# Up projections with the tokens stationary: half as many products, and the squared relu transposed on TensorE

## The chip, the core and the metric

The kernel runs on one core of a Trainium2 chip. The metric is the device time of one execution in microseconds (us); lower is better. Of the core's engines the text calls TensorE PE (its weight loads PEld, a row of their own in the profile), VectorE DVE, ScalarE ACT, and SyncE SP, which here issues the weight loads from memory.

## The reference

A decoder trunk of two layers on 256 tokens of 2048 channels, float32. Each layer adds a mixer (layer 0: window attention beside a state space scan; layer 1: dilated attention) and a feed-forward part to the residual. The change touches the feed-forward parts alone:

```python
D_MODEL = 2048
SEQ = 256
D_FF = 4 * D_MODEL

def squared_relu_mlp(h, w_up, w_down):
    u = jnp.einsum('bsd,df->bsf', h, w_up)
    return jnp.einsum('bsf,fd->bsd', jnp.square(jax.nn.relu(u)), w_down)

def reference(...):
    for layer in range(DEPTH):
        h = rms_norm(x, norm_mix[layer])
        ...
        h = rms_norm(x, norm_ffn[layer])
        x = x + squared_relu_mlp(h, w_up[layer], w_down[layer])
    return x
```

## The kernel before

All weights (some 416 MB) stream once through the core. A *unit* is 512 columns of one weight matrix against all 256 tokens; its inner dimension is cut into blocks of 128 rows, the *k-tiles*, and two k-tiles make a *chunk* of 512 KB. Every float32 operand is split into a high and a low part, and a product is the sum of three: high by high, high by low, low by high. For each chunk SP loads `wraw`, ACT copies it to `whi` (`high`), DVE subtracts to get `wlo` (`low`); both run a few chunks ahead (`RAW`, `AHEAD`). The loop in `run` goes through a list of (unit, chunk) in program order, so the order of the products is fixed by the order in which units are made: `up(0)`, `up(1)`, then for each i `up(2i)`, `up(2i+1)`, `down(i-1)`, and the last `down`. Each layer has 16 up units of 16 k-tiles, and 8 down steps of 4 units of 8 k-tiles.

A unit has two forms. In the plain form a block of 128 tokens is stationary and 512 weight columns move: 2 token blocks by 3 products, six products of 512 columns in a k-tile, and the result has the tokens on the partitions. With `flip=True` a block of 128 weight columns is stationary and the 256 tokens move: 4 blocks by 3 products, twelve of 256 columns, and the result has the weight columns on the partitions. In the profile's names the moving operand stands first: `acc<-hThi,whi` is a flipped product, `acc<-whi,hThi` a plain one.

The operand of the tokens is `hThi`/`hTlo` for an up unit (the residual, transposed and times the norm's gain, by `Norm.stripe`) and `uh`/`ul` for a down unit. The norm's factor of each token comes after the product. In a flipped unit the tokens lie along the free axis, so the factor must lie along it too: `Norm` with `rowwise=True` builds `rsb` by a product of a diagonal with ones. In a plain unit the factor is one number per partition (`rs_at`).

Work beside the products (`squared`, `stripe`, attention) is written as generators. `tick` runs before each k-tile and emits their next steps where the charged load allows it; `yield n` asks for a wait of n k-tiles. So a step's place in each engine's queue is set when the program is built. All engines issue in order. PSUM is held by `accs` (two tiles for each unit, two units alive) and `auxs` (four tiles for transposes and small products). Every recorded operation has the line 71, that of the helper which charges the load, so the tiles' names tell the rows apart.

Of the kernel before, what the change touches and what calls it, by code (L numbers as in the profile page):

```python
# [10 lines left out]
AF = mybir.ActivationFunctionType  # L11
# [28 lines left out]
def trunk(ctx: ExitStack, tc: tile.TileContext, x, norm_mix, norm_ffn, w_up, w_down, ab_w_in, ab_q_norm,  # L40
# [14 lines left out]
    spent = {"V": 0.0, "S": 0.0, "PE": 0.0}  # L55

    class Engine:
        """an engine whose instructions are charged roughly, so that work beside the products is spread evenly"""

        def __init__(self, engine, name, fixed, each):  # L60
            self.engine, self.name, self.fixed, self.each = engine, name, fixed, each
# [15 lines left out]
    def slot(name):  # L77
        return slots.tile([128, 4, T], F32R, name=name, tag="slot")
# [7 lines left out]
    def f32(ap):  # L86
        return ap.bitcast(F32)

    # ---------------------------------------------------------------- constants and parameters
    nc.scalar.preload_act_table(AF.Exp)  # L90
    cst = consts.tile([128, C_ALL], F32, name="cst")
    par0 = w4([32, 128], "par0")
# [51 lines left out]
        V.tensor_copy(cwT, p[:, 128:224])  # L144
        yield 4

    # ---------------------------------------------------------------- work beside the weight stream
    tasks = []
    done = set()
    clock = [0]  # L150

    def side(gen, label=None):
        """a step of gen is emitted between products; it yields how many row blocks to wait before the next"""
        tasks.append([clock[0], gen, label])

    def step(forced=False, skip=()):
# [38 lines left out]
    def free(ps):  # L195
        done.add(id(ps))

    # ---------------------------------------------------------------- small arithmetic
    def rsqrt(v, scale, shape, name):
        """1 / sqrt(v * scale + EPS), from a seed by the exponent and three Newton steps"""  # L200
        a = small.tile(shape, F32, name=name + "a", tag="rs_a")
        y = small.tile(shape, F32, name=name + "y", tag="rs_y")
        t = small.tile(shape, F32, name=name + "t", tag="rs_t")
        V.tensor_scalar(a, v, scale, EPS, op0=OP.mult, op1=OP.add)
        V.tensor_scalar(t.bitcast(I32), a.bitcast(I32), 1, None, op0=OP.logical_shift_right)
        V.tensor_scalar(y.bitcast(I32), t.bitcast(I32), -1.0, float(0x5F3759DF), op0=OP.mult, op1=OP.add)
        for _ in range(3):
            V.tensor_tensor(t, y, y, op=OP.mult)
            V.scalar_tensor_tensor(t, t, -0.5, a, op0=OP.mult, op1=OP.mult)
            V.scalar_tensor_tensor(y, t, 1.5, y, op0=OP.add, op1=OP.mult)  # L210
        return y

    def split(hi, lo, src, gain=None):
        """hi + lo = src (* gain), each of float32r's width"""
        if gain is None:
            S.activation(hi, src, AF.Copy)
            V.tensor_tensor(lo, src, f32(hi), op=OP.subtract)
        else:
            S.activation(hi, src, AF.Copy, scale=gain)
            V.scalar_tensor_tensor(lo, src, gain, f32(hi), op0=OP.mult, op1=OP.subtract)  # L220

    # ---------------------------------------------------------------- products with the weights
    units = []

    def unit(segs, ktiles, after, flip=False, needs={}):
        """rows of tokens by weight columns (flip: weight columns by tokens); ktiles: [(row block, operands)]"""
        units.append((segs, ktiles, after, flip, needs))

    def run():
# [90 lines left out]
                pending = after, ps  # L320
        pending[0](pending[1])

    # ---------------------------------------------------------------- the norm of the residual
    class Norm:
        """transposed, gained residual as (hi, lo) blocks; the row factors come after the product"""

        def __init__(self, row, rowwise):
            self.row, self.rowwise = row, rowwise
# [70 lines left out]
        def rsb2(self):  # L399
            return self.rsb[:, None, :].to_broadcast([128, 2, T])  # L400

    # ---------------------------------------------------------------- parts of attention
    def head_norm(nm, ps, n, name):
        """factors of the n heads of 64 columns in ps, the residual's factor included"""
        yield from until(("rs", nm.row))
        sq = w4([128, 2, n * 64], name + "sq")
        for t in range(2):
            S.activation(sq[:, t], ps[t][:, :n * 64], AF.Square, scale=nm.rs_at(t))
        yield 2
        s = small.tile([128, 2, n], F32, name=name + "s", tag="hn_s")  # L410
        V.tensor_reduce(s, sq.rearrange("p t (h e) -> p t h e", e=64), axis=AX.X, op=OP.add)
        y = rsqrt(s, 1.0 / 64, [128, 2, n], name)
        f = small.tile([128, 2, n], F32, name=name + "f", tag="hn_f")
        V.tensor_tensor(f, y, nm.rs[:, :, None].to_broadcast([128, 2, n]), op=OP.mult)
        yield 2
        return f

    def heads_T(nm, ps, gain, name, box):
        """eight heads: norm, then [(two heads, 64), tokens] blocks"""
        f = yield from head_norm(nm, ps, 8, name)  # L420
        qn = w4([128, 2, W], name + "n")
        for t in range(2):
            V.tensor_tensor(qn[:, t].rearrange("p (h e) -> p h e", e=64),
                            ps[t].rearrange("p (h e) -> p h e", e=64),
                            f[:, t, :, None].to_broadcast([128, 8, 64]), op=OP.mult)
        free(ps)
        yield 6
        qT = w4([128, 4, T], name + "T")
        for a in range(2):
            p = aux(name + "p")  # L430
            for b in range(2):
                for t in range(2):
                    PE.transpose(p[:, b * T + t * 128:b * T + (t + 1) * 128],
                                 qn[:, t, (2 * a + b) * 128:(2 * a + b + 1) * 128], ident)
            yield 1
            S.activation(qT[:, 2 * a:2 * a + 2], p.rearrange("p (b t) -> p b t", b=2), AF.Copy,
                         scale=gains[:, gain:gain + 1])
            yield 2
        box.append(qT)
        yield 1  # L440
# [1 line left out]
    BL = ((0, 128), (128, 384))  # L442

    def pair(b, pre, first, qT, kT, vs, hi, lo, mask, mult=None, sink=None, post=None):
        """two heads; blocks (q0,k0) (q1,k0) (q1,k1); kT(b), vs(t, head) pick the keys and values"""
        yield from until(pre)
        if first is not None:
            yield from until(first)
# [63 lines left out]
        split(hi()[:, b], lo()[:, b], o[:, :T])  # L512
        yield 1

    # ---------------------------------------------------------------- the residual's additions
    def add_stripe(ps, j, last=None):
        for t in range(2):
            r = res[:, t, j * W:(j + 1) * W]
# [11 lines left out]

            unit([(w, j * W, W)], ktiles, after, needs=needs if j == 0 else {})

    # ================================================================ layer 0, mixer
    win, wout = ab_w_in[0], ab_w_out[0]
    n0 = Norm(R_MIX, True)
    for j in range(NS):
# [39 lines left out]
        yield 2  # L576

    def steps(ps):
        """dt = softplus(dtx) with log1p(e) = 2 atanh(e / (2 + e)); the decays' prefix sums"""
        st = [128, 2, 32]  # L580
        yield from until(("rs", n0.row))
        V.tensor_scalar(rsh, n0.rs, 0.5, None, op0=OP.mult)
# [79 lines left out]
        unit([(win, AQ + u * W, W)], n0.ktiles(), lambda ps, u=u: swa(u, ps))  # L662

    def conv(ps, ch, y):
        """the causal convolution and 2 * silu of four blocks of channels"""
        pre = w4([128, 4, T], "pre")
        for a in range(2):
            V.tensor_tensor(pre[:, 2 * a:2 * a + 2], ps[a].rearrange("p (b t) -> p b t", b=2), n0.rsb2(), op=OP.mult)
# [40 lines left out]
    dxs, wts = {}, {}  # L709

    def decays(g):
        """(C B^T) * decay of both chunks, for the group's heads, source tokens on the partitions"""
        yield from until("steps")
        wt = []
        for c in range(2):
# [119 lines left out]
        else:  # L835
            unit([(win, AX0 + g * W, W)], n0.ktiles(), lambda ps, g=g: after_x(g, ps), flip=True)

    n1 = Norm(R_FFN, True)
    residual_units(wout, [(i, lambda i=i: (mixh[i // 4], mixl[i // 4], i % 4)) for i in range(24)],
                   {4 * i: ("mix", i) for i in range(6)}, n1)  # L840

    # ================================================================ the feed-forward part
    NB = FF // W

    def mlp(layer, nm, nxt, last=None):
# [2 lines left out]

        def squared(i, ps):
            yield from until(("rs", nm.row))  # L850
            u[i] = slot("uh"), slot("ul")
            ts = []
            for a in range(2):
                t = w4([128, 2, T], "relu")
                V.scalar_tensor_tensor(t, ps[a].rearrange("p (b t) -> p b t", b=2), 0.0, nm.rsb2(),
                                       op0=OP.max, op1=OP.mult)
                ts.append(t)
            free(ps)
            yield 2
            for a in range(2):  # L860
                S.activation(ts[a], ts[a], AF.Square)
                S.activation(u[i][0][:, 2 * a:2 * a + 2], ts[a], AF.Copy)
            yield 2
            for a in range(2):
                V.tensor_tensor(u[i][1][:, 2 * a:2 * a + 2], ts[a], f32(u[i][0][:, 2 * a:2 * a + 2]),
                                op=OP.subtract)
            yield 2

        def after_up(i, ps):
            side(squared(i, ps), ("u", layer, i))  # L870

        def up(i):
            unit([(wu, i * W, W)], nm.ktiles(), lambda ps: after_up(i, ps), flip=True, needs=nm.needs() if i == 0 else {})

        def down(i):
            kts = [(4 * (2 * i + b) + k, (lambda b=b, k=k: u[2 * i + b] + (k,))) for b in range(2) for k in range(4)]
# [12 lines left out]
    n2 = Norm(R_MIX + 16, False)  # L889
    mlp(0, n1, n2)  # L890

    # ================================================================ layer 1, mixer
    wqkv = c_w_qkv[0]
    oh, ol = [None] * 4, [None] * 4

# [43 lines left out]
    for g, i in ((0, 0), (0, 1), (1, 0), (1, 1), (2, 0), (3, 0), (2, 1), (3, 1)):  # L939
        parts[g][i]()  # L940

    n3 = Norm(R_FFN + 16, True)
    residual_units(c_w_o[0], [(i, (lambda i=i: (oh[i // 4], ol[i // 4], i % 4))) for i in range(16)],
                   {4 * g: ("o", g) for g in range(4)}, n3)

# [14 lines left out]


def _shapes():
    """arrays that follow from the shapes: identity, prefix triangle, masks, branch counts"""
    import numpy as np
    c = np.zeros((128, C_ALL), np.float32)
    i = np.arange(128)
# [35 lines left out]
```

## Time and profile before

| | |
|---|---|
| time, median of 3 executions | 2336.72 us (2336.21 to 2336.78) |
| profiled execution, first to last instruction (span) | 2334.6 us |
| PE busy | 2322.0 us, 99%, 14137 products |
| PEld busy | 2064.2 us, 88% |
| DVE busy | 1430.6 us, 61% |
| ACT busy | 1094.5 us, 47% |
| read from memory | 420.64 MB, 181 GB/s over the span |

The times are those of whole executions; the profiled one is given by its span, which leaves out what lies before the first and after the last instruction. A busy share is a mean over the whole span. Products on PE are pipelined, so the duration of one row overlaps the next: the rate is read from the starts.

### The profile page before, as it was taken

How to read it: one execution, taken by the hardware profiler on the slowest of the kernel's cores; microseconds unless marked ns; L12 is line 12 of the kernel's file. 1: busy time of each engine (PE TensorE's matmuls, PEld its weight loads, DVE VectorE, ACT ScalarE, POOL GpSimd, SP SyncE). 2: the span in 40 equal slices, each digit the busy share in tenths (PEclk: the TensorE clock that was granted, in tenths of full speed). 3: DMA queues.
4: the chain of work that ended last, by engine and by line, in shares of the span. 5: the costliest groups of instructions: out<-in, count | busy, mean ns of one | idle time of the engine just before them, and what ended most of it. 6: DMA issues, size and time to landing. Idle time of an engine off the chain costs nothing.

```text
span 2334.6 us, 35702 instructions
## 1 busy us (share of the span) xinstructions
PE 2322.0 (99%) x14137; PEld 2064.2 (88%) x14137; DVE 1430.6 (61%) x2188; ACT 1094.5 (47%) x1411; POOL 8.4 (0%) x20
## 2 busy tenths in 40 slices
PE   8999999999999999999999999999999999999999
PEld 7999988899899899899888778778989989989897
DVE  6779986555555555555566776755555555555554
ACT  5565545444344444444454555554444444344342
POOL 1000000000000000000000000000000000000000
PEclk9999999999999999999999999999999999999999
DMA  7546655565666656656555545456665665656654
GB/s 232 161 144 190 188 164 189 188 183 181 191 189 188 191 184 188 192 187 189 189 180 182 157 152 176 155 165 183 184 191 181 190 191 186 191 185 186 191 188 161
DMA packets 229223, 425.09 MB, mean 182 GB/s; under 512 B 15620, under 2 KB 26160, under 8 KB 229056
## 3 DMA queue, kind: packets, MB, share of 16 engines
q1 hardware_dynamic: 218976, 416.34, 57.7%
q10 hardware_dynamic: 9568, 6.34, 0.9%
q8 instruction: 110, 1.80, 0.3%
q14 instruction: 57, 0.47, 0.1%
q0 software_dynamic: 512, 0.15, 0.0%
HBM read 420.64 MB, written 2.13 MB: 181 GB/s over the span
## 4 chain that ended last, share of the span: by engine, by line
PE 99%; DMA 0%; DVE 0%; ACT 0%; SPq 0%; issue 0%; ACTq 0%
PE acc L71 94%; PE sc L71 1%; PE o L71 1%; PE pT L71 1%; PE yp L71 1%; PE xT L71 1%; DMA wraw<-in_ab_w_in_dram 0%; PE qp L71 0%; PE yo L71 0%; PE kp L71 0%; PE yT L71 0%; PE xtok L71 0%; PE hst L71 0%; DVE wlo L71 0%; ACT whi L71 0%; PE cbp L71 0%
## 5 line engine op out<-in xcount | busy, mean ns | idle before, releaser
L71 DVE TENSOR_TENSOR wlo<-wraw,whi 128x1024 fp32r<-128x1024 f32 (+1 forms) x792 | 962.5, 1218 | 685.1 <-PE acc L71 557.7
L71 ACT ACTIVATE whi<-wraw 128x1024 fp32r<-128x1024 f32 (+1 forms) x792 | 835.8, 1056 | 1085.4 <-PE acc L71 981.9
L71 PE MATMUL acc<-hThi,whi 128*128 128x256 f32 x2432 | 692.5, 285 | 0.0
L71 PE MATMUL acc<-hThi,wlo 128*128 128x256 f32 x2432 | 688.1, 283 | 0.0
L71 PE MATMUL acc<-hTlo,whi 128*128 128x256 f32 x2432 | 688.1, 283 | 0.0
L71 PEld LDWEIGHTS acc<-hThi,whi 128*128 128x128 f32 x2432 | 466.6, 192 | 4.0 <-issue 3.3
L71 PEld LDWEIGHTS acc<-hTlo,whi 128*128 128x128 f32 x2432 | 466.7, 192 | 1.6 <-issue 1.0
L71 PEld LDWEIGHTS acc<-hThi,wlo 128*128 128x128 f32 x2432 | 466.6, 192 | 0.0
L71 PE MATMUL acc<-whi,uh 128*128 128x512 f32 x1024 | 399.1, 390 | 0.0
L71 PE MATMUL acc<-wlo,uh 128*128 128x512 f32 x1024 | 398.5, 389 | 0.0
L71 PE MATMUL acc<-whi,ul 128*128 128x512 f32 x1024 | 398.4, 389 | 0.0
L71 PE MATMUL acc<-whi,hThi 128*128 128x512 f32 (+1 forms) x608 | 243.8, 401 | 2.8 <-ACT hThi L71 2.8
L71 PE MATMUL acc<-whi,hTlo 128*128 128x512 f32 (+1 forms) x608 | 235.9, 388 | 0.3 <-DVE hTlo L71 0.3
L71 PE MATMUL acc<-wlo,hThi 128*128 128x512 f32 (+1 forms) x608 | 235.3, 387 | 0.0
L71 PEld LDWEIGHTS acc<-whi,ul 128*128 128x128 f32 x1024 | 192.2, 188 | 40.1
L71 PEld LDWEIGHTS acc<-whi,uh 128*128 128x128 f32 x1024 | 192.3, 188 | 39.3
L71 PEld LDWEIGHTS acc<-wlo,uh 128*128 128x128 f32 x1024 | 192.3, 188 | 39.2
L71 DVE TENSOR_TENSOR res<-acc,res 128x512 f32<-128x512 f32 x144 | 98.8, 692 | 78.1 <-PE acc L71 78.1
L71 PEld LDWEIGHTS acc<-whi,hThi 128*128 128x128 f32 x608 | 115.4, 190 | 29.5 <-issue 5.9
L71 PEld LDWEIGHTS acc<-whi,hTlo 128*128 128x128 f32 x608 | 115.1, 189 | 24.4 <-DVE hTlo L71 0.9
L71 PEld LDWEIGHTS acc<-wlo,hThi 128*128 128x128 f32 x608 | 115.4, 190 | 21.5 <-issue 1.0
L71 PE MATMUL acc<-whi,mixh 128*128 128x512 f32 x192 | 75.6, 394 | 0.0
(198 smaller groups left out, 1444.5 us busy)
## 6 DMA issues: line engine op xcount, KB each, us to landing
wraw<-in_w_up_dram SPq DMA_DIRECT2D x256, 512.0 KB, 3.7
wraw<-in_w_down_dram SPq DMA_DIRECT2D x256, 512.0 KB, 4.4
wraw<-in_ab_w_in_dram SPq DMA_DIRECT2D x96, 512.0 KB, 3.7
wraw<-in_c_w_qkv_dram SPq DMA_DIRECT2D x96, 512.0 KB, 3.8
wraw<-in_ab_w_out_dram SPq DMA_DIRECT2D x48, 512.0 KB, 3.9
wraw<-in_c_w_o_dram SPq DMA_DIRECT2D x32, 512.0 KB, 3.9
wt<-cumd ACTq DMA_DIRECT2D x8, 512.0 KB, 6.9
res<-in_x_dram SPq DMA_DIRECT2D x4, 512.0 KB, 5.0
```

Source lines behind the costliest of these rows:

```text
L71: return f(out, *a, **k)
```

## The change

Up units lose `flip=True`. The squared relu is then formed with the tokens on the partitions: ACT applies relu and the token's factor to both PSUM tiles, DVE squares, PE transposes the result in two groups of four 128x128 blocks into `uT`, and ACT and DVE split that into `uh` and `ul`. The norms ahead of the feed-forward parts no longer build `rsb`.

```diff
-    n1 = Norm(R_FFN, True)
+    n1 = Norm(R_FFN, False)
...
         def squared(i, ps):
             yield from until(("rs", nm.row))
-            u[i] = slot("uh"), slot("ul")
-            ts = []
-            for a in range(2):
-                t = w4([128, 2, T], "relu")
-                V.scalar_tensor_tensor(t, ps[a].rearrange("p (b t) -> p b t", b=2), 0.0, nm.rsb2(),
-                                       op0=OP.max, op1=OP.mult)
-                ts.append(t)
+            r = w4([128, 2, W], "relu")
+            for t in range(2):
+                S.activation(r[:, t], ps[t], AF.Relu, scale=nm.rs_at(t))
             free(ps)
             yield 2
+            V.tensor_tensor(r, r, r, op=OP.mult)
+            yield 3
+            u[i] = slot("uh"), slot("ul")
             for a in range(2):
-                S.activation(ts[a], ts[a], AF.Square)
-                S.activation(u[i][0][:, 2 * a:2 * a + 2], ts[a], AF.Copy)
-            yield 2
-            for a in range(2):
-                V.tensor_tensor(u[i][1][:, 2 * a:2 * a + 2], ts[a], f32(u[i][0][:, 2 * a:2 * a + 2]),
-                                op=OP.subtract)
-            yield 2
+                p = aux("uT")
+                for b in range(2):
+                    for t in range(2):
+                        PE.transpose(p[:, b * T + t * 128:b * T + (t + 1) * 128],
+                                     r[:, t, (2 * a + b) * 128:(2 * a + b + 1) * 128], ident)
+                yield 1
+                p = p.rearrange("p (b t) -> p b t", b=2)
+                split(u[i][0][:, 2 * a:2 * a + 2], u[i][1][:, 2 * a:2 * a + 2], p)
+                yield 2
...
-            unit([(wu, i * W, W)], nm.ktiles(), lambda ps: after_up(i, ps), flip=True, needs=nm.needs() if i == 0 else {})
+            unit([(wu, i * W, W)], nm.ktiles(), lambda ps: after_up(i, ps), needs=nm.needs() if i == 0 else {})
...
-    n3 = Norm(R_FFN + 16, True)
+    n3 = Norm(R_FFN + 16, False)
```

On PE, in the up unit that follows the fifth one of layer 0 (`up(5)`), the products of one k-tile stood like this before; one token operand moves against blocks of `whi` and `wlo`:

```order
L71 MATMUL acc_6502<-hThi_4184,whi_6410 128x256
L71 MATMUL acc_6502<-hTlo_4185,whi_6410 128x256
L71 MATMUL acc_6502<-hThi_4184,wlo_6436 128x256
L71 MATMUL acc_6503<-hThi_4184,whi_6410 128x256
L71 MATMUL acc_6503<-hTlo_4185,whi_6410 128x256
L71 MATMUL acc_6503<-hThi_4184,wlo_6436 128x256
```

In the changed kernel the same unit, around the end of its sixth k-tile, reads (`relu` is the squared relu of the fifth unit, `cst` the identity):

```order
L71 MATMUL acc_6048<-whi_6027,hThi_4428 128x512
L71 MATMUL acc_6048<-wlo_6041,hThi_4428 128x512
L71 MATMUL acc_6048<-whi_6027,hTlo_4429 128x512
L71 MATMUL uT_6097<-cst_81,relu_6049 128x128 x4
L71 MATMUL acc_6047<-whi_6027,hThi_4428 128x512
L71 MATMUL acc_6047<-wlo_6041,hThi_4428 128x512
L71 MATMUL acc_6047<-whi_6027,hTlo_4429 128x512
```

A k-tile's twelve products have become six, and the first four transposes stand behind 36 products of the unit that follows; the second four stand 18 products later, and so it is after all 32 up units. All other instructions of PE keep their place between the products, but for the two `rsb` pairs that go.

On ACT, around the same unit's end, before (a `relu` row here squares what DVE made):

```order
L71 ACTIVATE whi_6538<-wraw_6438 128x1024
L71 ACTIVATE relu_6506<-relu_6506 128x512
L71 ACTIVATE uh_6504<-relu_6506 128x512
L71 ACTIVATE relu_6508<-relu_6508 128x512
L71 ACTIVATE uh_6504<-relu_6508 128x512
L71 ACTIVATE whi_6572<-wraw_6468 128x1024
```

and in the changed kernel:

```order
L71 ACTIVATE whi_6045<-wraw_5989 128x1024
L71 ACTIVATE relu_6049<-acc_5901,rs32_4979 128x512
L71 ACTIVATE relu_6049<-acc_5902,rs32_4979 128x512
L71 ACTIVATE whi_6068<-wraw_6007 128x1024
L71 ACTIVATE whi_6087<-wraw_6025 128x1024
L71 ACTIVATE whi_6112<-wraw_6043 128x1024
L71 ACTIVATE uh_6095<-uT_6097 128x512
L71 ACTIVATE whi_6132<-wraw_6066 128x1024
L71 ACTIVATE uh_6095<-uT_6134 128x512
L71 ACTIVATE whi_6157<-wraw_6085 128x1024
```

ACT still has four instructions for the unit, but two of them now wait for PE's transposes, each with a `whi` queued behind it.

On DVE, before (the first two rows read the unit's PSUM tiles):

```order
L71 SCALAR_TENSOR_TENSOR relu_6506<-acc_6260,rsb_5194 128x512
L71 SCALAR_TENSOR_TENSOR relu_6508<-acc_6261,rsb_5194 128x512
L71 TENSOR_TENSOR wlo_6534<-wraw_6408,whi_6500 128x1024
L71 TENSOR_TENSOR wlo_6568<-wraw_6438,whi_6538 128x1024
L71 TENSOR_TENSOR ul_6505<-relu_6506,uh_6504 128x512
L71 TENSOR_TENSOR ul_6505<-relu_6508,uh_6504 128x512
```

and in the changed kernel:

```order
L71 TENSOR_TENSOR wlo_6064<-wraw_5989,whi_6045 128x1024
L71 TENSOR_TENSOR relu_6049<-relu_6049 128x1024
L71 TENSOR_TENSOR wlo_6083<-wraw_6007,whi_6068 128x1024
L71 TENSOR_TENSOR wlo_6108<-wraw_6025,whi_6087 128x1024
L71 TENSOR_TENSOR ul_6096<-uT_6097,uh_6095 128x512
L71 TENSOR_TENSOR wlo_6128<-wraw_6043,whi_6112 128x1024
L71 TENSOR_TENSOR ul_6096<-uT_6134,uh_6095 128x512
```

The reading of PSUM moved to ACT, one square of 1024 columns came in, and the two subtractions moved behind the transposes, with one `wlo` between them.

## Rows read from the trace of the kernel before

**Rows 1.** The page: span, PE and PEld (busy, share, count), PE and its granted clock over 40 slices (tenths), the bytes from memory and their rate, and the shares of the chain of work that ended last.

```profile
span 2334.6 us, 35702 instructions
PE 2322.0 (99%) x14137; PEld 2064.2 (88%) x14137; DVE 1430.6 (61%) x2188; ACT 1094.5 (47%) x1411; POOL 8.4 (0%) x20
PE   8999999999999999999999999999999999999999
PEclk9999999999999999999999999999999999999999
HBM read 420.64 MB, written 2.13 MB: 181 GB/s over the span
PE 99%; DMA 0%; DVE 0%; ACT 0%; SPq 0%; issue 0%; ACTq 0%
```

**Rows 2.** The chain of work that ended last, its last piece: start, length, what, count.

```profile
1636.76 693.90 PE acc L71 x4416
```

**Rows 3.** The page's costliest groups: count, busy us and mean ns of one, idle time before them and its main releaser.

```profile
L71 DVE TENSOR_TENSOR wlo<-wraw,whi 128x1024 fp32r<-128x1024 f32 (+1 forms) x792 | 962.5, 1218 | 685.1 <-PE acc L71 557.7
L71 ACT ACTIVATE whi<-wraw 128x1024 fp32r<-128x1024 f32 (+1 forms) x792 | 835.8, 1056 | 1085.4 <-PE acc L71 981.9
```

**Rows 4.** PE in order of time (start us, duration us): the borders of a block of two up units (714.08 to 760.15) and of the down step behind it (760.15 to 803.70), layer 0.

```profile
713.85 0.39 PE L71 MATMUL acc<-whi,ul 128*128 128x512 f32 x1
714.08 0.28 PE L71 MATMUL acc<-hThi,whi 128*128 128x256 f32 x1
...
760.03 0.28 PE L71 MATMUL acc<-hThi,wlo 128*128 128x256 f32 x1
760.15 0.40 PE L71 MATMUL acc<-whi,uh 128*128 128x512 f32 x1
...
803.47 0.39 PE L71 MATMUL acc<-whi,ul 128*128 128x512 f32 x1
803.70 0.28 PE L71 MATMUL acc<-hThi,whi 128*128 128x256 f32 x1
```

**Rows 5.** Groups of instructions by form within 714.0 to 760.1, then within 760.12 to 803.6: count, busy us and mean ns of one. One of three products is shown of each; the other two have the same counts and means.

```profile
L71 PE MATMUL acc<-hThi,wlo 128*128 128x256 f32 x128 | 36.2, 283 | 0.0
...
L71 PE MATMUL acc<-whi,uh 128*128 128x512 f32 x64 | 24.9, 389 | 0.0
```

**Rows 6.** Busy time of the engines in stretches (PE, PEld, DVE, ACT, POOL, each with a count; granted clock, DMA share, GB/s): the same up block, the same down step, the projections of layer 1's attention.

```profile
714.00:760.10 46.10, 46.10 (x386) 46.06 (x385) 23.45 (x23) 19.14 (x20) 0.00 (x0) 1.00 0.60 183
760.10:803.60 43.50, 43.50 (x194) 36.03 (x194) 25.86 (x27) 19.21 (x20) 0.00 (x0) 1.00 0.62 194
1208.40:1512.00 303.60, 303.60 (x1498) 243.38 (x1497) 208.76 (x554) 160.56 (x232) 0.00 (x0) 1.00 0.53 167
```

**Rows 7.** PE in order of time in layer 1's attention, where plain units with `hThi` run and two groups of four transposes (`qp`) stand between their products.

```profile
1458.93 0.39 PE L71 MATMUL acc<-whi,hTlo 128*128 128x512 f32 x1
1459.16 0.60 PE L71 MATMUL qp<-cst,qn 128*128 128x128 f32 x4
1459.52 0.48 PE L71 MATMUL acc<-whi,hThi 128*128 128x512 f32 x1
...
1463.51 0.39 PE L71 MATMUL acc<-whi,hTlo 128*128 128x512 f32 x1
1463.73 0.60 PE L71 MATMUL qp<-cst,qn 128*128 128x128 f32 x4
1464.09 0.47 PE L71 MATMUL acc<-whi,hThi 128*128 128x512 f32 x1
...
1472.13 0.39 PE L71 MATMUL acc<-whi,hTlo 128*128 128x512 f32 x1
```

**Rows 8.** Stretches between those groups, of instructions on `acc` alone (PE, PEld, DVE, ACT with counts; clock, DMA share, GB/s); the count of PEld is that of the products between.

```profile
1459.40:1463.70 4.30, 4.18 (x18) 3.30 (x18) 0.00 (x0) 0.00 (x0) 1.00 0.69 248
1463.70:1472.30 8.60, 8.41 (x37) 6.68 (x36) 1.28 (x2) 0.00 (x0) 1.00 0.63 186
```

**Rows 9.** The group of those transposes by form, mean ns of one.

```profile
L71 PE MATMUL qp<-cst,qn 128*128 128x128 f32 x48 | 7.2, 272 | 0.0
```

**Rows 10.** PE in order of time around the product that builds `rsb` in layer 0's feed-forward part.

```profile
511.26 0.28 PE L71 MATMUL acc<-hThi,wlo 128*128 128x256 f32 x1
511.38 0.59 PE L71 MATMUL rsb<-diag,ones 128*128 128x256 f32 x2
511.62 0.47 PE L71 MATMUL acc<-hThi,whi 128*128 128x256 f32 x1
511.93 0.28 PE L71 MATMUL acc<-hTlo,whi 128*128 128x256 f32 x1
512.04 0.28 PE L71 MATMUL acc<-hThi,wlo 128*128 128x256 f32 x1
```

**Rows 11.** Tiles' instructions (count, duration ns min/median/max): DVE reading PSUM and ACT in the old squared relu, DVE on 1024 columns in SBUF, ACT with a token's factor from PSUM, DVE's subtraction.

```profile
L71 DVE SCALAR_TENSOR_TENSOR relu<-acc,rsb x64: 681/692/693, 513.5 to 2243.6; 128x512 f32<-128x512 f32 x64
L71 ACT ACTIVATE relu<-relu x64: 611/614/616, 515.7 to 2245.6; 128x512 f32<-128x512 f32 x64
L71 ACT ACTIVATE uh<-relu x64: 632/632/633, 516.4 to 2246.3; 128x512 fp32r<-128x512 f32 x64
L71 DVE TENSOR_TENSOR ul<-relu,uh x64: 681/685/690, 519.3 to 2247.9; 128x512 fp32r<-128x512 f32 x64
L71 DVE TENSOR_TENSOR z<-z,dx x4: 1218/1218/1225, 232.9 to 360.4; 128x1024 f32<-128x1024 f32 x4
L71 ACT ACTIVATE v<-acc,rs x10: 348/690/690, 42.7 to 1515.3; 128x512 f32<-128x512 f32 x8, 128x128 f32<-128x128 f32 x2
```

**Rows 12.** DVE in order of time at the end of an up unit (its products end at the middle of the block of Rows 4, 737.11): start, duration, idle before and its releaser.

```profile
736.59 1.41 DVE L71 SCALAR_TENSOR_TENSOR relu<-acc,rsb 128x512 f32<-128x512 f32 x2 [0.88 <-PE acc L71]
```

**Rows 13.** Loads from memory: count, KB each, median us from issue to landing.

```profile
wraw<-in_w_up_dram SPq DMA_DIRECT2D x256, 512.0 KB, 3.7
wraw<-in_w_down_dram SPq DMA_DIRECT2D x256, 512.0 KB, 4.4
```

**Rows 14.** The start of layer 1's feed-forward part: its first products on PE, then DVE's last piece of the norm's last stripe, which the thirteenth k-tile reads.

```profile
1612.26 0.28 PE L71 MATMUL acc<-hThi,whi 128*128 128x256 f32 x1
...
1624.80 0.87 DVE L71 SCALAR_TENSOR_TENSOR hTlo<-xT,gains,hThi 128x256 fp32r<-128x256 f32 x2
```

## The prediction

> **What bounds the kernel now.** I read the page first: engines, slices, chain. PE is busy 99% of the span in nearly every slice, its granted clock stands at the upper of its two levels, 2.4 GHz, throughout, and the chain that ended last is PE for 99% [rows 1]. "Busy" alone would not tell whether PE waits, since durations overlap, so I looked at the pieces of the chain: from 1636.76 to the end 4416 products follow one another for 693.90 us with nothing else in between [rows 2]. The other engines wait for PE: ACT's `whi` 981.9 us, DVE's `wlo` 557.7 us [rows 3]. So in the feed-forward parts the time is the number of PE instructions times the distance between their starts, and the change is to be priced in that coin.
>
> That distance is read from the borders of blocks. Two up units, 384 flipped products of 256 columns (three groups of 128), take 714.08 to 760.15, 46.07 us: 0.1200 us each. The down step behind them, 192 products of 512 columns (three groups of 64), takes 43.55 us: 0.2268 us each [rows 4, 5]. The mean durations (283 and 389 ns) are no rates: they overlap. A product of twice the columns costs 0.2268 where two cost 0.2400, so each product carries some 0.013 us that doesn't depend on its columns. Put another way: 256 more columns cost 0.1068 us, which is 256 columns at 2.4 GHz, and 0.0132 us of each start is left over.
>
> **The change, part by part.**
>
> *The products.* There are 2 x 16 up units of 16 k-tiles. Flipped they are 12 products per k-tile, 6144 in all: 6144 x 0.1200 = 737.1 us. Plain they are 3072: 3072 x 0.2268 = 696.8 us. Gain 40.3 us. The columns that pass through PE are the same in both; the gain is all in the 3072 starts that go. That the plain form with `hThi` stationary runs at the same distance as the down step is seen in layer 1's attention: between two groups of transposes 18 and 36 products (the counts of PEld in [rows 8]) lie within 4.58 and 8.62 us [rows 7], which leaves no room for a slower one.
>
> The Trainium skill speaks against this term: its page "TensorE: Matmul & The Clock Gate", section "Back-to-back issue gap", gives an isolated distance of N/2.4 + 2.5 ns. By it two products of 256 cost 218.3 ns and one of 512 costs 215.8, so the gain would be an estimated 7.7 us and, with the other terms below, the kernel some 22 us slower. The trace doesn't agree: its fixed part is 13 ns, not 2.5, on both widths [rows 4].
>
> *The transposes.* Each unit now has two groups of four, 64 groups. The nearest rows could hardly be nearer: `qp`, four transposes of 128x128 float32 between plain products of the same form [rows 7]. One is shown with a mean of 272 ns [rows 9], yet four are through in 0.36 us, from 1459.16 to the next product at 1459.52. The price is what the group adds to the stream, including the first products behind it, whose distance is longer (1463.73, 1464.09). From 1458.93 to 1463.51 there are 18 products and one group: 4.58 - 18 x 0.2268 = 0.50 us. From 1463.51 to 1472.13 there are 36 and one: 8.62 - 8.16 = 0.46 us. A unit will have just such a pair, 0.96 us; 32 of them cost 30.5 us. Bounds: all as the cheaper, 29.1; all as the dearer, 31.9 us; further out, 0.60 us for each, the busy time in the group's own row [rows 7], 38.4 us.
>
> *The row factor.* Two `rsb` pairs go. Around one, three products take 0.78 us (511.26 to 512.04) where they take 0.36, so a pair costs 0.42 us [rows 10]; 0.8 us for both layers. That relu no longer waits for `rsb` shortens no chain, since PE waited for neither.
>
> *ACT and DVE.* ACT per unit: before 2 x 614 + 2 x 632 = 2.5 us; after, four of 512 columns from PSUM, the nearest row 690 ns (`v`), 2.8 us. DVE per unit: before 2 x 692 + 2 x 685 = 2.75 us; after, a square at 1.22 us and two subtractions at 0.69: 2.6 us [rows 11]. Both are priced at nothing: in an up block DVE has 23.45 of 46.10 us and ACT 19.14 [rows 6], and in the attention stage PE stays full with DVE at 209 of 304 us.
>
> *The new wait.* PE now waits for the squared relu before each first group; behind that wait stand all its products. When is the square ready? DVE's `relu` began at 736.59, before its unit's end at 737.11 [rows 12], because it needs only the half that is done first, some 0.2 us after that half. In the plain form the first token block is done three products earlier than the second, so ACT's two instructions end about 0.2 + 0.69 = 0.9 us after the unit. DVE has one `wlo` (1.22 us, [rows 3]) ahead of the square; if that starts at the unit's end the square is done about 2.5 us after it. The first transposes stand 36 products later, 8.2 us. Margin 5.7 us. Behind the first `uh`, which waits for the transposes (to about 8.8 us), stands a `whi` for the eighth chunk of this unit, needed after 7 x 2.72 = 19.0 us; with 0.69 us for `uh` and 1.06 of its own [rows 3, 11] it is done at 10.6. Behind `ul` stands a `wlo` for the seventh chunk, needed at 16.3 us and done by about 11.4. So I take zero, and keep a late square as a rival.
>
> *Next in line.* If PE speeds up, does the weight stream follow? A unit of 4.19 MB will take 96 x 0.2268 + 0.96 = 22.7 us, 185 GB/s, between the 183 of an up block and the 194 that the down step had with PE full [rows 6]; in one short stretch it reached 248 [rows 8]. Loads land after 3.7 to 4.4 us [rows 13], less than two chunks. At a layer's start, the norm's last stripe is done at 1624.80 + 0.87 = 1625.67, and its first reader will come 12 x 6 x 0.2268 = 16.3 us after 1612.26, at 1628.6 [rows 14]: 2.9 us are left, and the stripe's steps are placed by k-tiles and move forward with them.
>
> **The sum.** -40.3 - 0.8 + 30.5 = -10.6 us against the span of 2334.6: 2324.0 us. The median lies 2.1 us above the span, so I predict 2326.1 us, 0.45% less. With the bounds of the transposes, 29.1 to 31.9, it is 2324.7 to 2327.5; the borders are read to 0.01 us, so each distance is uncertain by some 0.1 us in 384 products, which over the 16 blocks is 1 to 2 us more on either side.
>
> **The rivals.** 0.2% of the time, 4.7 us, is about what a measurement of this kernel can tell from no change.
>
> 1. *The columns are the price* (slower). If the time went by columns streamed and not by starts, the products would gain nothing and the groups would be added: 2336.7 - 0.8 + 30.5 = 2366 us. The mechanism decides from a fixed part below (30.5 - 0.8) / 3072 = 9.7 ns per product; the rows give 13 [rows 4], and the two widths run under the same clock. A fixed part of a fifth of the measured one would end here too; 2%. (The Trainium skill's rule from "TensorE: Matmul & The Clock Gate" is a case of it; with its 7.7 us of gain the time would be an estimated 2358.7.)
>
> 2. *PE waits at the first group* (slower). The place is `uT`, on the square of `relu`; it decides from 10.6 / 32 = 0.33 us of wait per unit, which needs the square 6.0 us later than I worked out. A square that slips by three chunks of 2.72 us, as when DVE's queue is held by a `wlo` whose `wraw` is late, gives 2.5 us in each unit: 2326 + 80 = 2406 us. Against it: DVE itself waited 557.7 us for PE [rows 3]. 4%.
>
> 3. *The weights don't follow* (no change). If up units could not run faster than the 183 GB/s they ran at, the transposes would fill PE's waits and the blocks would keep their 46.07 us: 2335.9 us. For it: the mean of 181 is near [rows 1]. Against it: 194 with PE full in the next block [rows 6]. 4%.
>
> 4. *Dear groups* (no change). At 0.60 us each: 2326.1 + 7.9 = 2334.0 us. For it: the first group behind a wait from another engine is the dearer of the two in rows 7. Against it: both `qp` groups have such a wait behind them and are counted in full. 5%.
>
> **How the numbers follow.** My forecast has 85%. Rivals 3 and 4 end within 0.2% (2332.0 to 2341.4) and 1 and 2 above it. So faster 0.85, the same 0.09, slower 0.06. The range is that of the forecast, with the uncertainty of the distances and a part of the way to the dear groups: 2322.5 to 2330.
>
> **What the trace will show.** Right: up products `acc<-whi,hThi` 0.227 us apart; a block of two up units from its first product to the down step's first in about 45.5 us instead of 46.07; two `uT` rows of four per unit, each adding 0.46 to 0.50 us; no idle time of PE put down to DVE `relu`; granted clock at the top level; the chain of PE still without a piece of another engine in the feed-forward parts. Wrong: idle time before `uT`, products further apart than 0.227 us in up units, ACT's `whi` waiting for DMA instead of PE, or groups near 0.6 us.

## The result and the profile after

The changed kernel takes 2324.63 us (median of 5, 2324.33 to 2325.13), the kernel before, run beside it, 2336.21 (2336.09 to 2336.78). The ratio is 0.9950 with a 95% interval of 0.9937 to 0.9962; 11.6 us less. 2326.1 was forecast, with a range of 2322.5 to 2330. In a later set of runs it took 2324.81 us beside 2336.28.

The page of the changed kernel, the lines that answer to [rows 1] and [rows 3]:

```profile
span 2322.7 us, 30056 instructions
PE 2310.5 (99%) x11317; PEld 1928.3 (83%) x11317; DVE 1425.4 (61%) x2150; ACT 1100.2 (47%) x1411; POOL 8.4 (0%) x20
PEclk9999999999999999999999999999999999999999
PE acc L71 93%; PE uT L71 1%; PE sc L71 1%; PE o L71 1%; PE pT L71 1%; PE yp L71 1%; PE xT L71 1%; DMA wraw<-in_ab_w_in_dram 0%; PE qp L71 0%; PE yo L71 0%; PE kp L71 0%; PE xtok L71 0%; PE yT L71 0%; PE hst L71 0%; DVE wlo L71 0%; ACT whi L71 0%
...
L71 DVE TENSOR_TENSOR wlo<-wraw,whi 128x1024 fp32r<-128x1024 f32 (+1 forms) x792 | 962.3, 1218 | 611.3 <-PE acc L71 524.1
L71 ACT ACTIVATE whi<-wraw 128x1024 fp32r<-128x1024 f32 (+1 forms) x792 | 836.7, 1058 | 950.6 <-PE acc L71 831.9
```

PE has 2820 instructions fewer, which is -3072 products, -4 for `rsb` and +256 transposes. It is as full as before, at the same granted clock, and `wlo` and `whi` still wait for PE (524.1 and 831.9 us, [rows 3]: 557.7 and 981.9). So the bound has not moved; its work has become shorter. Each product has a load of its own (x11317 in both rows), and PEld fell from 88% to 83% with them.

PE in order of time: the borders of a block of two up units (from 711.61) and of the down step behind it (756.08 to 800.54), where [rows 4] has 46.07 and 43.55 us, and in between two groups of transposes:

```profile
711.61 0.39 PE L71 MATMUL acc<-whi,hThi 128*128 128x512 f32 x1
...
739.94 0.39 PE L71 MATMUL acc<-whi,hTlo 128*128 128x512 f32 x1
740.17 0.60 PE L71 MATMUL uT<-cst,relu 128*128 128x128 f32 x4
740.52 0.48 PE L71 MATMUL acc<-whi,hThi 128*128 128x512 f32 x1
...
744.50 0.39 PE L71 MATMUL acc<-whi,hTlo 128*128 128x512 f32 x1
744.73 0.60 PE L71 MATMUL uT<-cst,relu 128*128 128x128 f32 x4
745.08 0.48 PE L71 MATMUL acc<-whi,hThi 128*128 128x512 f32 x1
...
755.85 0.39 PE L71 MATMUL acc<-whi,hTlo 128*128 128x512 f32 x1
756.08 0.39 PE L71 MATMUL acc<-whi,uh 128*128 128x512 f32 x1
...
800.54 0.39 PE L71 MATMUL acc<-whi,hThi 128*128 128x512 f32 x1
```

The blocks now take 44.47 and 44.46 us, 192 products and two groups each: up and down cost PE the same. The two groups of the block's second unit stand in the down step. From 739.94 to 744.50 there are 18 products and one group: 4.56 - 18 x 0.2267 = 0.48 us, as at `qp` in [rows 7].

What the new wait has to spare is seen on ACT and DVE around the end of the first of those units, 711.61 + 96 x 0.2267 = 733.37 (start, duration, in brackets the idle time before and its releaser):

```profile
732.89 1.37 ACT L71 ACTIVATE relu<-acc,rs 128x512 f32<-128x512 f32 x2 [0.98 <-PE acc L71]
...
733.40 1.22 DVE L71 TENSOR_TENSOR wlo<-wraw,whi 128x1024 fp32r<-128x1024 f32 x1 [1.50 <-PE acc L71]
734.54 1.22 DVE L71 TENSOR_TENSOR relu<-relu 128x1024 f32<-128x1024 f32 x1
```

ACT's relu ends 0.9 us and the square 2.4 us after the unit. The transposes follow at 740.17, 6.8 us after it and not 8.2: here the text ahead of the result was wrong, on which more below.

### The profile page after: what moved, and what is told of

Read it like the earlier page. It is cut to its first block, busy times and chain, and to the rows that moved or that the text cites. A ratio compares the mean times of both kernels' runs of the same rounds, so it can differ in the third digit from the quotient of the medians.

```text
span 2322.7 us, 30056 instructions
## 1 busy us (share of the span) xinstructions
PE 2310.5 (99%) x11317; PEld 1928.3 (83%) x11317; DVE 1425.4 (61%) x2150; ACT 1100.2 (47%) x1411; POOL 8.4 (0%) x20
## 4 chain that ended last, share of the span: by engine, by line
PE 99%; DMA 0%; DVE 0%; ACT 0%; SPq 0%; issue 0%; ACTq 0%
PE acc L71 93%; PE uT L71 1%; PE sc L71 1%; PE o L71 1%; PE pT L71 1%; PE yp L71 1%; PE xT L71 1%; DMA wraw<-in_ab_w_in_dram 0%; PE qp L71 0%; PE yo L71 0%; PE kp L71 0%; PE xtok L71 0%; PE yT L71 0%; PE hst L71 0%; DVE wlo L71 0%; ACT whi L71 0%
## 5 line engine op out<-in xcount | busy, mean ns | idle before, releaser
L71 DVE TENSOR_TENSOR wlo<-wraw,whi 128x1024 fp32r<-128x1024 f32 (+1 forms) x792 | 962.3, 1218 | 611.3 <-PE acc L71 524.1
L71 ACT ACTIVATE whi<-wraw 128x1024 fp32r<-128x1024 f32 (+1 forms) x792 | 836.7, 1058 | 950.6 <-PE acc L71 831.9
L71 PE MATMUL acc<-whi,hThi 128*128 128x512 f32 (+1 forms) x1632 | 645.9, 396 | 2.6 <-ACT hThi L71 2.6
L71 PE MATMUL acc<-whi,hTlo 128*128 128x512 f32 (+1 forms) x1632 | 634.7, 389 | 0.3 <-DVE hTlo L71 0.3
L71 PE MATMUL acc<-wlo,hThi 128*128 128x512 f32 (+1 forms) x1632 | 634.0, 388 | 0.0
L71 PEld LDWEIGHTS acc<-whi,hThi 128*128 128x128 f32 x1632 | 307.6, 188 | 68.0 <-issue 5.8
L71 PEld LDWEIGHTS acc<-whi,hTlo 128*128 128x128 f32 x1632 | 307.4, 188 | 64.8 <-DVE hTlo L71 0.9
L71 PEld LDWEIGHTS acc<-wlo,hThi 128*128 128x128 f32 x1632 | 307.9, 189 | 60.2 <-issue 1.0
L71 PE MATMUL acc<-hThi,whi 128*128 128x256 f32 x384 | 112.3, 293 | 0.0
L71 PE MATMUL acc<-hThi,wlo 128*128 128x256 f32 x384 | 108.5, 283 | 0.0
L71 PE MATMUL acc<-hTlo,whi 128*128 128x256 f32 x384 | 108.5, 283 | 0.0
L71 PEld LDWEIGHTS acc<-hThi,whi 128*128 128x128 f32 x384 | 73.5, 191 | 3.4 <-issue 3.3
```

The source lines that it names most:

```text
L71: return f(out, *a, **k)
```

## The experiments

Ten are variants of the changed kernel, and one is the changed kernel once more. The first four price its terms.

**The count of starts: `e1_halves`.** Each plain up product is cut in two. Up units get this branch, the others keep theirs:

```diff
+                if flip == "cut":
+                    for t in range(2):
+                        h, l = xh[:, t * 128:(t + 1) * 128], xl[:, t * 128:(t + 1) * 128]
+                        for c0, c1 in ((0, 256), (256, W)):
+                            o, wh, wl = ps[t][:, c0:c1], hi[:, k, c0:c1], lo[:, k, c0:c1]
+                            PE.matmul(o, h, wh, start=first and c0 == 0, stop=False, skip_group_check=True)
+                            PE.matmul(o, h, wl, start=False, stop=False, skip_group_check=True)
+                            PE.matmul(o, l, wh, start=False, stop=last, skip_group_check=True)
```

> The changed kernel, but each up product of 512 weight columns is cut into two of 256: the tokens stay stationary, the stationary block is loaded anew for each half, and the count of starts is the old one (12 per k-tile). My theory (a start costs 13 ns beside its columns, whichever operand is stationary): 0.120 us from start to start, 3072 starts more at 13.3 ns, 40.9 us more than the changed kernel's 2324.6: 2365.5 us. Rival (the gain comes from which operand is stationary, tokens instead of weight columns, not from the count): no change, 2324.6 us.

Measured: 2364.57 us (2364.03 to 2364.66), 39.9 us above the changed kernel. The distance is that of the old flipped products:

```profile
719.95 0.28 PE L71 MATMUL acc<-whi,hThi 128*128 128x256 f32 x1
720.07 0.28 PE L71 MATMUL acc<-wlo,hThi 128*128 128x256 f32 x1
720.19 0.28 PE L71 MATMUL acc<-whi,hTlo 128*128 128x256 f32 x1
```

So which operand stands still plays no part; the count of starts does. (Each start here has a weight load of its own, so the 13 ns are those of a start with its load.) That the products' term is some 40 us, and why, is shown for these widths.

The groups of transposes are a little cheaper among these halves. Two products ahead of a group, with the groups:

```profile
748.63 0.28 PE L71 MATMUL acc<-whi,hTlo 128*128 128x256 f32 x1
748.75 0.60 PE L71 MATMUL uT<-cst,relu 128*128 128x128 f32 x4
...
753.37 0.28 PE L71 MATMUL acc<-whi,hTlo 128*128 128x256 f32 x1
753.50 0.60 PE L71 MATMUL uT<-cst,relu 128*128 128x128 f32 x4
```

Between the two products lie 36 starts and one group: 4.74 - 36 x 0.120 = 0.42 us, 0.05 less than among products of 512. 36 of the 64 groups stand in up units (the others in down steps), so the 39.9 us hold a saving of some 1.8 us, and the starts alone cost an estimated 41.7 us.

**How far the rule reaches: `e2_uneven`.** The same with `((0, 384), (384, W))`.

> As the run with two halves, but cut into 384 and 128 columns: the same count of starts, the same columns. My theory (fixed part plus 0.4167 ns per column): 173.3 + 66.7 = 240.0 ns per pair, as with the halves, 2365.5 us. Rival (a start can't follow the one before it faster than a weight load allows; the transposes' starts, 0.109 us apart with 128 columns each, are that floor): 173.3 + 109 = 282 ns per pair against 226.7, 3072 x 56 ns = 171 us more than the changed kernel: 2496 us.

Measured: 2510.36 us (2510.11 to 2510.91). My theory fell, by 145 us, and the rival came within 14. PE in order of time (start, duration):

```profile
559.69 0.39 PE L71 MATMUL acc<-whi,hThi 128*128 128x384 f32 x1
559.91 0.34 PE L71 MATMUL acc<-wlo,hThi 128*128 128x384 f32 x1
560.09 0.34 PE L71 MATMUL acc<-whi,hTlo 128*128 128x384 f32 x1
560.27 0.23 PE L71 MATMUL acc<-whi,hThi 128*128 128x128 f32 x1
560.33 0.28 PE L71 MATMUL acc<-wlo,hThi 128*128 128x128 f32 x1
560.44 0.27 PE L71 MATMUL acc<-whi,hTlo 128*128 128x128 f32 x1
560.55 0.40 PE L71 MATMUL acc<-whi,hThi 128*128 128x384 f32 x1
560.78 0.34 PE L71 MATMUL acc<-wlo,hThi 128*128 128x384 f32 x1
```

Busy times in a stretch of it (PE, PEld, DVE, ACT, POOL, then granted clock, DMA share, GB/s):

```profile
560.00:572.00 12.00, 12.00 (x85) 12.00 (x84) 5.21 (x5) 3.84 (x5) 0.00 (x0) 1.00 0.47 135
```

The products of 384 columns stand 0.175 us apart, as the fixed part and the columns say (160 + 13 ns). For those of 128 the rule gives 0.067 us: the first is followed after 0.06, the other two only after 0.11, and the product of 384 after them needs 0.23 before the next may start. The six take 0.86 us where three of 512 take 0.68; 1024 x 0.183 = 187 us, the measured rise. PEld is busy for all of the 12 us. That alone doesn't tell that the loads set the pace, since it was as busy in the old up block at 0.120 us (46.06 of 46.10 us [rows 6]). What speaks for it is that the distance no longer goes with the moving columns. In layer 0's mixer, products of 64 columns (`yp`) run one behind the other, each with a load of a full 128x128 block, here in the changed kernel's trace:

```profile
214.79 1.89 PE L71 MATMUL yp<-xdt,wt 128*128 128x64 f32 x16
216.49 0.37 PE L71 MATMUL acc<-hThi,whi 128*128 128x256 f32 x1
```

16 starts take 1.70 us, 0.106 each, where 13 ns and the columns would give 0.04. Nor is a start as such held to 0.11, since one followed after 0.06. The loads are the reading that fits both; no run changed the loads alone, so it is argued and not shown. The Trainium skill, page "TensorE: Matmul & The Clock Gate", section "LDWEIGHTS (loading the stationary operand)", gives P / 1.2 ns for P columns, an estimated 107 ns for 128; the 0.11 us here agree. So the "13 ns beside the columns" of the prediction holds from 256 to 512 columns and may not be carried below: with a load for each product, 256 columns at 0.120 us stand just above that floor.

**The groups: `e3_no_transposes` and `e4_twice`.**

```diff
-                p = aux("uT")
-                for b in range(2):
-                    for t in range(2):
-                        PE.transpose(...)
                 yield 1
-                p = p.rearrange("p (b t) -> p b t", b=2)
+                p = r[:, a].rearrange("p (b t) -> p b t", b=2)
```

> The changed kernel without its 256 transposes: the split reads the squared relu as it lies (this leaves the transposition out of the computation). My theory: the 64 groups cost 0.472 us each in PE's stream, 30.2 us, so 2294.4 us. Rival (the transposes partly fill time in which PE would wait for ACT or DVE): a smaller fall, above 2300 us, with idle time of PE or longer distances between products in the trace.

Measured: 2293.91 us (2293.66 to 2294.45), 30.7 us less than the changed kernel. The last piece of the chain of work is unbroken again, as in [rows 2]:

```profile
1598.55 689.56 PE acc L71 x3042
```

So the transposes fill no idle time; all of their price is on the path.

```diff
-                for b in range(2):
+                for b in (0, 1, 0, 1):
                     for t in range(2):
                         PE.transpose(...)
```

> The changed kernel with every group of four transposes made twice in a row (eight to a group, the second four overwrite the first with the same). My theory: a transpose costs its distance of 0.109 us and a group some 0.036 us beside that, so 256 more cost 27.9 us: 2352.5 us. Rival (the price is one per group, for leaving and entering the stream of products, as the longer distances behind a group suggest): clearly less, near the changed kernel's 2324.6 us. Rival (a transpose costs its duration, 272 ns): 69.6 us more, 2394 us.

Measured: 2352.10 us (2351.73 to 2352.88), 27.5 us above the changed kernel, 0.107 us for each of 256 more transposes. A group of eight in its place:

```profile
751.14 0.40 PE L71 MATMUL acc<-whi,hTlo 128*128 128x512 f32 x1
751.38 1.03 PE L71 MATMUL uT<-cst,relu 128*128 128x128 f32 x8
752.17 0.47 PE L71 MATMUL acc<-whi,hThi 128*128 128x512 f32 x1
```

From the group's start to the next product 0.79 us, against 0.35 for four: the price goes by transposes, at 0.11 us each. Neither the duration (272 ns, [rows 9]) nor a price per group alone is what is paid.

**Place: `e5_at_12`, `e6_at_6`, `e9_at_12_true`.** These move the first transposes nearer to the unit's end. The names of the first two are wrong, since I had counted a unit of 288 columns as a full one: they stand at 6 and at 0 products, the third at 12. The edit of `e5_at_12` is shown; `e6_at_6` has no `yield` in either place, `e9_at_12_true` has `yield 1` in both.

```diff
             free(ps)
-            yield 2
             V.tensor_tensor(r, r, r, op=OP.mult)
-            yield 3
+            yield 1
```

> The changed kernel with its first transposes 12 products behind the unit's end instead of 36 (relu and square are emitted in one step, the transposes one k-tile later). The squared relu is done 2.2 to 2.4 us after the unit's end, and 12 products take 2.72 us. My theory (a group costs its 0.472 us wherever it stands, as long as its operand is ready): 2324.6 us, no idle time of PE. Rival (PE pays something for a wait that is met only just): up to 0.5 us per unit, 16 us, 2341 us.

Measured: 2353.78 us (2353.08 to 2354.28), against both expectations, because of the miscount. At 6 products the transposes are reached 1.36 us after the unit's end (at 831.65, so the unit ended at 830.29), and the square is done at 832.45, 2.2 us after it. DVE's square and PE in order of time, with the idle time before and its releaser:

```profile
831.22 1.23 DVE L71 TENSOR_TENSOR relu<-relu 128x1024 f32<-128x1024 f32 x1 [2.39 <-ACT relu L71]
831.42 0.39 PE L71 MATMUL acc<-whi,hTlo 128*128 128x512 f32 x1
832.50 0.66 PE L71 MATMUL uT<-cst,relu 128*128 128x128 f32 x4 [0.68 <-DVE relu L71]
832.91 0.47 PE L71 MATMUL acc<-whi,hThi 128*128 128x512 f32 x1
```

1.08 us lie between the starts instead of 0.23. With the transposes a little further apart that is 0.9 us in each of 32 units, 29 us: the measured rise, and what was worked out for 6 products in the next run's expectation.

> The changed kernel with its first transposes 6 products (1.36 us) behind the unit's end, before the squared relu is done (2.2 to 2.4 us). My theory: PE stands for the difference, about 0.95 us, in each of 32 units, and nothing else fills it, 30 us more: 2355 us, with idle time before uT put down to DVE's relu. Rival (the products behind the transposes are pulled ahead, or ACT and DVE, which run ahead, make it up): 2324.6 us.

Measured: 2418.89 us (2417.71 to 2419.72), 94 us above the changed kernel; at 0 products, so the number in the text was for another place. The wait itself is 2.43 - 0.23 = 2.20 us; with 0.06 us for transposes that stand a little further apart behind it, as in `e5_at_12`, it comes to some 72 us in 32 units. The other 22 us come from the clock. Three stretches around one of these waits, busy times of the engines with the granted clock third from the end:

```profile
557.00:562.20 5.20, 3.16 (x16) 2.35 (x15) 2.38 (x2) 2.43 (x3) 0.00 (x0) 1.00 0.60 184
562.30:565.70 3.40, 3.40 (x10) 2.75 (x9) 1.82 (x2) 1.54 (x2) 0.00 (x0) 0.50 0.01 2
566.00:580.00 14.00, 14.00 (x65) 11.56 (x64) 6.73 (x6) 5.92 (x6) 0.00 (x0) 1.00 0.58 188
```

PE in order of time in them:

```profile
559.39 0.39 PE L71 MATMUL acc<-whi,hTlo 128*128 128x512 f32 x1
561.82 0.75 PE L71 MATMUL uT<-cst,relu 128*128 128x128 f32 x4 [2.04 <-DVE relu L71]
...
563.23 0.63 PE L71 MATMUL acc<-whi,hTlo 128*128 128x512 f32 x1
563.66 0.63 PE L71 MATMUL acc<-whi,hThi 128*128 128x512 f32 x1
```

Behind the wait the clock stands at 0.50, the lower of its two levels, and the products 0.43 us apart. Such a stretch follows the wait in 13 of the 32 units. Over the whole span the granted clock was 0.991 on average; 0.009 x 2416 = 22 us.

> The two runs before this with early transposes stood at 6 and at 0 products behind the unit's end, not at 12 and 6 as their expectations say (the first projection unit of the kernel has fewer columns, which I had counted as a full one; in the changed kernel the groups stand at 30 and 48, not 36 and 54). This run has them at 12: 2.72 us behind the unit's end. My theory (PE waits only for what is late; in the run at 6 products the square was done 2.4 us after the unit's end): no wait, 2324.6 us. Rival (the square moves later too, because its emission moves behind a wlo on DVE): done after up to 3.5 us, 0.8 us of wait per unit, 2350 us.

Measured: 2324.66 us (2323.90 to 2325.19), the changed kernel's own time, and no row of PE waiting for DVE's `relu`. DVE's square and the first two transposes in order of time:

```profile
733.75 1.22 DVE L71 TENSOR_TENSOR relu<-relu 128x1024 f32<-128x1024 f32 x1 [2.39 <-ACT relu L71]
```

```profile
735.32 0.39 PE L71 MATMUL acc<-whi,hTlo 128*128 128x512 f32 x1
735.55 0.38 PE L71 MATMUL uT<-cst,relu 128*128 128x128 f32 x2
```

The square is done at 734.97, 0.6 us before it is wanted. That margin does as well as the 4.4 us of the changed kernel.

**Room in the weight stream: `e8_two_products`.**

```diff
+                if flip == "two":
+                    for t in range(2):
+                        PE.matmul(ps[t], xh[:, t * 128:(t + 1) * 128], hi[:, k], start=first, stop=False)
+                        PE.matmul(ps[t], xh[:, t * 128:(t + 1) * 128], lo[:, k], start=False, stop=last)
```

Up units get this branch; the third product, low part of the tokens by high part of the weights, is left out in them.

> The changed kernel with two of three products in up units (low part of the tokens by high part of the weights is left out of the computation), to ask how fast the weights could follow. An up unit then needs 64 x 0.2267 + 0.94 = 15.45 us on PE for 4.19 MB, 271 GB/s. My theory (the stream is not what sets the pace in the changed kernel, and has room): below 2176 us; if PE stays the bound even here, 1024 x 0.2267 = 232 us less, 2092 us; if the stream then binds at the 232 to 248 GB/s that short stretches showed, 16.9 to 18.1 us per unit, 2139 to 2176 us. Rival (the stream gives no more than the 183 to 194 GB/s seen so far): 21.6 to 22.9 us per unit, 2290 to 2325 us.

Measured: 2093.64 us (2092.99 to 2094.36), 231.0 us less than the changed kernel, for 1024 products: 0.2256 us each, so PE set the pace even here. Its page:

```profile
PE 2078.6 (99%) x10293; PEld 1735.5 (83%) x10293; DVE 1421.5 (68%) x2150; ACT 1092.3 (52%) x1411; POOL 8.4 (0%) x20
```

The busy times of a stretch over up and down (granted clock, DMA share and GB/s at its end), and then the largest waits for loads (us, times, the longest):

```profile
600.00:690.00 90.00, 90.00 (x408) 74.56 (x407) 60.41 (x57) 48.96 (x52) 0.00 (x0) 1.00 0.73 235
```

```profile
ACT whi L71 <- DMA wraw<-in_w_up_dram: 89.2, 105, 3.1
ACT whi L71 <- DMA wraw<-in_w_down_dram: 53.0, 55, 2.5
```

At 235 GB/s over 90 us, ACT begins to wait for loads, but PE stays full. The rival of a stream bound near 190 GB/s is out.

**One group instead of two: `e7_merged`, `e10_changed_again`, `e11_merged_again`.** All eight transposes of a unit stand together, each half in a PSUM tile of its own.

```diff
+            pp = []
             for a in range(2):
                 p = aux("uT")
                 ...
-                yield 1
-                split(...)
-                yield 2
+                pp.append(p)
+            yield 1
+            for a in range(2):
+                split(..., pp[a])
+                yield 2
```

> The changed kernel with a unit's two groups of four transposes as one group of eight, at the place of the first. My theory: a group costs 0.036 us beside its transposes, so 32 groups fewer gain 1.2 us: 2323.4 us, less than a measurement tells, seen in the span alone. Rival (price per group): 32 x 0.2 us or more, 2318 us or less. Rival (the two splits in a row hold up ACT or DVE): above 2326 us.

Measured: 2323.15 us (2322.94 to 2323.47). That is 1.5 us below the changed kernel's 2324.63, near my theory's 1.2 us and in neither rival's range; since the two could differ by their chips, both were run once more on one chip.

> The changed kernel itself, unaltered, beside the merged version on one chip: 2324.6 us.

> The version with one group of eight transposes per unit once more, to be compared with the changed kernel of the same chip. My theory (0.036 us per group saved, 32 groups): 1.2 us below it, 2323.4 us, with the median of the one outside the other's range. Rival (the difference between the two earlier medians was the chips'): no difference.

Measured, side by side: the changed kernel 2324.81 us (2324.46 to 2325.00), the merged version 2323.09 (2322.79 to 2323.20), ratio to the kernel before 0.9943 (0.9930 to 0.9955). The merged version is 1.7 us below the changed one; 32 groups fewer, 0.05 us each. The intervals of the two ratios overlap (the changed kernel's is 0.9937 to 0.9962), so this rests on the times themselves: five of each, whose ranges don't touch, and a distance of the same size the first time. The medians of the merged version lie below those of both kernels.

## Why the prediction was right, and where it was off

*The bound.* PE's starts set the time, before and after; the `whi` and `wlo` rows above and the unbroken chain of `e3_no_transposes` show it.

*The products, -40.3 us.* Right in size and reason for the widths at hand: `e1_halves` gives 39.9 us back by doubling the starts. The reason was put too broadly: the constant of 13 ns doesn't hold for 128 columns, where the weight loads seem to bind (`e2_uneven`). Nothing in the sum rested on that.

*The transposes, +30.5 us.* `e3_no_transposes` measured 30.7: right, and for the reason given, since the nearest rows had the very form.

*The row factor, -0.8 us.* Not tried alone; too small to tell.

*The sum, -10.6 us.* Measured -11.6. With the distances of the changed kernel's own trace, 0.2267 us for a product and (44.47 - 192 x 0.2267) / 2 = 0.47 us for a group, the same sum is -(737.1 - 696.4) - 0.8 + 30.1 = -11.4 us, so what was missing is the last digit of two distances, times 3072 and 64. The terms as the experiments undid them, one at a time, give -39.9 + 30.7 - 0.8 = -10.0; with the groups' saving in `e1_halves` added to the starts, the estimate is -41.7 + 30.7 - 0.8 = -11.8. Of the 1.5 us between 2326.1 and 2324.6, the other 0.5 us is the base: the forecast started from 2336.7, and the kernel before took 2336.2 beside the changed one.

*ACT and DVE at nothing.* Right. ACT took 598 ns, not 690, to copy 512 columns from PSUM (`uh<-uT`), which hid nothing and cost nothing.

*The new wait.* Zero, as said, but the step was wrong in one number. The groups stand behind 30 and 48 products of the following unit, not behind 36 and 54; so it also reads in the part on the change, whose sixth k-tile is the fifth. The margin was 4.4 us, not 5.7. The square's moment, 2.5 us after the unit's end, was right (2.4, and 2.2 where no `wlo` stands ahead of it), and the rival's mechanism is real: at 6 products it costs 29 us, at 0 it costs 94.

*What the trace would show.* "About 45.5 us" for two up units was wrong: 44.47. The second unit's groups stand in the down step, which rose from 43.55 to 44.46; I had left all four in the up block. For the pair, the sum's share was (-40.3 + 30.5) / 16 = -0.61 us, from 89.62 to 89.01; it is 88.93.

*The rivals.* Columns as the price: out (`e1_halves`). Weights that don't follow: out (`e8_two_products`). Dear groups at 0.60 us: out (0.47 to 0.48). The wait: real, but 4.4 us away.

## What to carry to other kernels

Where PE is full, count its starts and read the distance between them from the borders of long blocks, not from durations: at these widths two products of 256 columns cost 13 ns more than one of 512, and 3072 of them outweigh 256 transposes. A transpose between products costs 0.11 us and some 0.05 us for each group, so put them together, and behind enough products that their operand is ready: a margin of 0.6 us was enough, and waits of 2 us cost 72 us by themselves and another 22 us in the clock that fell behind 13 of the 32.

## What the runs showed that I had not expected

With a load of a full 128x128 block for each product, starts came no closer than about 0.11 us on average, so products of 64 or 128 columns cost nearly as much as those of 256 (0.12 us); a product of 384 columns behind them pays the rest (0.23 instead of 0.175 us).

Waits of PE of 2.0 us after dense work were followed in 13 of 32 units by a stretch at the lower clock (0.50 from 562.30 to 565.70, products 0.43 us apart), while waits of 0.7 us in `e5_at_12` left the mean clock at 1.000.
